# The values of attention groups 2 and 3 as seven block products, and the pooling tiles ahead of these groups' queries and keys

## The chip, the cores and the metric

The kernel runs on one core of one Trainium2 chip. The metric is the device time of one execution in microseconds (us), as the median of several executions. The profile is one execution recorded by the hardware profiler. Engines: PE is TensorE (matrix products), DVE is VectorE, ACT is ScalarE, POOL is GpSimd, SP is SyncE (it issues most of the transfers).

## The reference

One decoder block on 512 tokens of width 1024 in float32: a SwiGLU, a token-mixing layer, a second SwiGLU, each after a norm that is scaled and shifted by a conditioning vector (`w_ada`). The change lies in the token-mixing layer:

```python
proj = u @ w_in                       # u: 512 x 1024
p, q, k, v, gate_logits = split(proj) # widths 256, 768, 768, 768, 2048
y_pool = multiscale_pool(p, ...)      # trailing means over 2, 4, 8, 16 tokens, minus the token
q, k = rope(q), rope(k)               # three head groups of 4 heads x 64, dilations 1, 4, 16
outs, lses = zip(*(dilated_window_attention(q[g], k[g], v[g]) for g in range(3)))
y_attn = sum over groups of softmax(lses)[g] * outs[g]
gates = sigmoid(gate_logits)
merged = g_pool * (y_pool @ w_pool_branch) + g_attn * (y_attn @ w_attn_branch)
return merged @ w_out
```

The reference's head groups are 0, 1 and 2; the words "groups 2 and 3" mean the second and third of them.

## The kernel before

**Products in three parts.** A float32 operand x is held as hi + lo (both in the format fp32r), and a product is three: hi·hi, lo·hi, hi·lo. The activations u are split once (`UH`, `UL`, eight tiles of 128 features by 512 tokens). Weights come in chunks of 128 x 1024 (512 KB) in the order of `plan`. SP issues their transfer into one of three buffers `raw`; ACT writes the high part `whi` (L377) and DVE the low part `wlo` (L389) into a ring. `look`, called ahead of each tile or product, fetches and splits some steps ahead. `take` hands the split chunk to PE.

**Tiles and blocks.** A plain tile of 128 outputs by 512 tokens is 24 matmuls with 512 columns into one bank of PSUM (`mm_tile`, L421 to L423). `blocks` does four such chunks as a 2x2 block product with seven products in place of eight, each of 24 matmuls with 256 columns (L749 to L751 in `gate_duo`). For that it forms sums of weights: two by DVE (`make`, L312) and two by an accumulating transfer that POOL issues (`add`, L320), and sums of blocks of u. Three banks A, B, C take the products: the first result, in A, is copied by ACT to C before the third product goes on accumulating in A.

**The mixing layer (`mix`).** Order of its weight chunks: q and k of group 1, v of group 1; then eight tiles of q and k of groups 2 and 3; two pooling tiles; four chunks of v of groups 2 and 3; then the gates in pairs ("groups" (6), (0), (2), (4) of `GROUPS`, each with seven block products) with the merge products; then `w_out`.

- Each q or k tile is followed by `rope_a`: ACT copies the bank (L1397), SP issues four transfers that swap rows (L1400), DVE multiplies the bank by the cosines (L1401) and so frees it. `rope_b` (two DVE instructions, L1419 and L1423) follows one tile later.
- A row of `w_ada` is one DVE instruction (L448). Such rows are spread over the tiles (`bg`).
- The attention runs beside the tiles (`hooks`): scores (L1456, 16 or 8 matmuls), then on DVE four masked maxima (L1472), on ACT four exponentials (L1477); a step later transposes on PE (L1489) that ACT copies (L1492); a step later the products with the values (L1507) that DVE copies (L1513, L1515). Group 1 has four such steps, here A0 to A3, groups 2 and 3 together four, B0 to B3.
- A pooling tile ends in `pool_diff`: ACT copies the bank (L1582), POOL forms the trailing means (L1588 to L1597).
- The values of groups 2 and 3 are four chunks of 128 tokens by 512 features: 24 matmuls of 512 columns each (L1765 to L1767), copied by DVE (L1768). B1 to B3 run in these.
- Sums of blocks of u for the first gate pair (`mix_sums`): a transfer copies `UH`, one of POOL adds `UL` (L1319, L1322), DVE adds two more (L1326) and combines them (L1337, L1338), ACT and DVE split them (L1330, L1334).
- `gate_duo` for the gate pair 6 stands between the values and the merge. After its fifth product come `pool_map` (L1608, whose result ACT and DVE read, L1612 and L1613) and `at_fT` (L1547). `settle` (L427) is a matmul of 240 columns ahead of some products whose result is not used.

The instructions of each engine run in the order in which the program emits them; there is no planner beside the calls in `mix`.

## Time and profile before

| | us |
|---|---|
| median of 3 runs (lowest to highest) | 968.51 (967.84 to 969.17) |
| the profiled execution | 969.99 |
| its span from first to last instruction | 968.2 |
| values of groups 2 and 3 with their attention steps | 450.95 to 483.98 in the span |
| gate pair 6, seven products | 483.98 to 507.9 |

A row of the timeline reads: start in us, duration in us, engine, line, operation, result<-operands, shapes, count, and in brackets the idle time before it with what ended it. Durations of one engine overlap, so the time that an instruction takes from its queue is the distance from its start to the next start. The busy shares of the page: PE 99%, DVE 87%, ACT 56%, POOL 9%.

### The profile page before, as it was taken

How to read it: one execution, taken by the hardware profiler on the slowest of the kernel's cores; microseconds unless marked ns; L12 is line 12 of the kernel's file. 1: busy time of each engine (PE TensorE's matmuls, PEld its weight loads, DVE VectorE, ACT ScalarE, POOL GpSimd, SP SyncE). 2: the span in 40 equal slices, each digit the busy share in tenths (PEclk: the TensorE clock that was granted, in tenths of full speed). 3: DMA queues.
4: the chain of work that ended last, by engine and by line, in shares of the span. 5: the costliest groups of instructions: out<-in, count | busy, mean ns of one | idle time of the engine just before them, and what ended most of it. 6: DMA issues, size and time to landing. Idle time of an engine off the chain costs nothing.

```text
span 968.2 us, 18169 instructions
## 1 busy us (share of the span) xinstructions
PE 958.5 (99%) x7296; PEld 899.9 (93%) x7296; DVE 840.3 (87%) x1237; ACT 539.3 (56%) x813; POOL 89.8 (9%) x106
## 2 busy tenths in 40 slices
PE   9999999999999999999999999999999999999997
PEld 7888999999999899778889998998999999999997
DVE  7989999899998778787897877989799888989886
ACT  5443666665755553444565453365666747566655
POOL 0000110101010003005510000000101000110002
PEclk9999999999999999999999999999999999999999
DMA  9857785776768648766457445723757666665632
GB/s 353 283 178 257 197 239 156 202 212 153 219 176 246 171 148 238 239 206 188 90 141 199 124 126 207 243 73 104 194 141 198 170 157 167 172 171 143 169 83 88
DMA packets 54087, 174.71 MB, mean 180 GB/s; under 512 B 7793, under 2 KB 10481, under 8 KB 53746
## 3 DMA queue, kind: packets, MB, share of 16 engines
q1 hardware_dynamic: 44416, 141.29, 44.2%
q0 software_dynamic: 9008, 31.72, 18.1%
q8 instruction: 57, 0.93, 0.4%
q10 hardware_dynamic: 578, 0.53, 0.2%
q14 instruction: 28, 0.23, 0.1%
HBM read 135.36 MB, written 2.24 MB: 142 GB/s over the span
## 4 chain that ended last, share of the span: by engine, by line
PE 84%; DVE 7%; DMA 4%; issue 2%; ACT 1%; POOL 0%; SPq 0%; POOLq 0%; DVEq 0%; ACTq 0%
PE bank L750 13%; PE bank L749 12%; PE bank L751 12%; PE bank L421 7%; PE bank L422 7%; PE bank L423 7%; PE bank L1109 4%; PE bank L1108 4%; PE bank L1110 4%; DVE wlo L389 2%; PE bank L2119 2%; PE bank L2121 1%; PE bank L2123 1%; DMA v<-wada 1%; DMA cs<-wada 1%
## 5 line engine op out<-in xcount | busy, mean ns | idle before, releaser
L389 DVE TENSOR_TENSOR wlo<-raw,whi 128x1024 fp32r<-128x1024 f32 (+3 forms) x150 | 166.4, 1118 | 37.7 <-ACT whi L377 37.5
L749 PE MATMUL bank<-UH,whi 128*128 128x256 f32 x672 | 185.7, 276 | 0.0
L750 PE MATMUL bank<-UL,whi 128*128 128x256 f32 x672 | 185.6, 276 | 0.0
L751 PE MATMUL bank<-UH,wlo 128*128 128x256 f32 x672 | 185.6, 276 | 0.0
L389 DVE TENSOR_TENSOR wlo<-X,whi 128x1024 fp32r<-128x1024 f32 (+3 forms) x133 | 142.2, 1082 | 17.8 <-ACT whi L377 17.6
L377 ACT ACTIVATE whi<-raw 128x1024 fp32r<-128x1024 f32 (+3 forms) x150 | 142.6, 964 | 22.1 <-DMA raw<-wf1o 8.4
L377 ACT ACTIVATE whi<-X 128x1024 fp32r<-128x1024 f32 (+3 forms) x133 | 123.0, 946 | 51.0 <-DVE X L312 46.1
L750 PEld LDWEIGHTS bank<-UL,whi 128*128 128x128 f32 x672 | 126.3, 188 | 0.0
L749 PEld LDWEIGHTS bank<-UH,whi 128*128 128x128 f32 x672 | 126.1, 188 | 0.2
L751 PEld LDWEIGHTS bank<-UH,wlo 128*128 128x128 f32 x672 | 126.2, 188 | 0.0
L751 PE MATMUL bank<-SH,wlo 128*128 128x256 f32 x408 | 112.7, 276 | 0.2 <-DVE wlo L389 0.2
L749 PE MATMUL bank<-SH,whi 128*128 128x256 f32 x408 | 112.6, 276 | 0.0
L750 PE MATMUL bank<-SL,whi 128*128 128x256 f32 x408 | 112.6, 276 | 0.0
L421 PE MATMUL bank<-UH,whi 128*128 128x512 f32 (+1 forms) x272 | 93.0, 342 | 0.0
L422 PE MATMUL bank<-UL,whi 128*128 128x512 f32 (+1 forms) x272 | 92.0, 338 | 0.0
L423 PE MATMUL bank<-UH,wlo 128*128 128x512 f32 (+1 forms) x272 | 91.8, 337 | 0.0
L751 PEld LDWEIGHTS bank<-SH,wlo 128*128 128x128 f32 x408 | 76.6, 188 | 0.4 <-DVE wlo L389 0.4
L749 PEld LDWEIGHTS bank<-SH,whi 128*128 128x128 f32 x408 | 76.6, 188 | 0.0
L750 PEld LDWEIGHTS bank<-SL,whi 128*128 128x128 f32 x408 | 76.6, 188 | 0.0
L1108 PE MATMUL bank<-HI,whi 128*128 128x256 f32 x224 | 61.8, 276 | 0.0
L1109 PE MATMUL bank<-HK,whi 128*128 128x256 f32 x224 | 61.8, 276 | 0.0
L1110 PE MATMUL bank<-HI,wlo 128*128 128x256 f32 x224 | 61.8, 276 | 0.0
(406 smaller groups left out, 2410.9 us busy)
## 6 DMA issues: line engine op xcount, KB each, us to landing
raw<-wmix SPq DMA_DIRECT2D x44, 512.0 KB, 4.3
raw<-wf1i SPq DMA_DIRECT2D x32, 512.0 KB, 5.9
raw<-wf2i SPq DMA_DIRECT2D x30, 512.0 KB, 4.3
ada<-wada SPq DMA_DIRECT2D x23, 512.0 KB, 5.2
X<-raw POOLq DMA_DIRECT2D x23, 512.0 KB, 6.0
xs<-wada SPq DMA_DIRECT2D x17, 512.0 KB, 5.3
X<-wf2i SPq DMA_DIRECT2D x14, 512.0 KB, 4.5
X<-wf1i SPq DMA_DIRECT2D x11, 512.0 KB, 4.6
```

The source lines that it names most:

```text
L377: self.nc.scalar.activation(self.hi[:, y], r[:, x], AF.Copy)
L389: self.nc.vector.tensor_tensor(self.lo[:, y], r[:, x], self.hi[:, y], op=OP.subtract)
L421: M(ps, hi, uh, start=start, stop=False)
L422: M(ps, hi, ul, start=False, stop=False)
L423: M(ps, lo, uh, start=False, stop=stop)
L749: M(o, hi, uh, start=start and p == 0 and k == 0, stop=False, skip_group_check=True)
L750: M(o, hi, ul, start=False, stop=False, skip_group_check=True)
L751: M(o, lo, uh, start=False, stop=k == 3, skip_group_check=True)
L1108: M(o, hi, uh, start=start and m % 2 == 0 and k == 0, stop=False, skip_group_check=True)
L1109: M(o, hi, ul, start=False, stop=False, skip_group_check=True)
L1110: M(o, lo, uh, start=False, stop=k == 1, skip_group_check=True)
L2119: M(b, hi, self.UH[k], start=k == 0, stop=False)
```

## The change

1. **Order of chunks.** The two pooling tiles come ahead of the q and k tiles of groups 2 and 3, which are called n0 to n7 here. Their POOL work uses other scratch space.
2. **Values by blocks.** The four v chunks become one `blocks` with seven products of 24 matmuls, 256 columns each (`value_duo`, lines L1834 to L1836 of the changed kernel). u is the stationary operand, the weights move. The bank of n7 is its C.
3. **Sums of u.** All four sums are formed by DVE (L1323), beside the tiles n4 to n7, and serve the values and all gates. The copying and adding transfers are gone.
4. **Attention steps.** B0 starts in the middle of value product 2 (counted from 0), B1 in product 4, B2 in product 6, B3 in the gate product 1; the rest follows in gate products 3 and 5.
5. **Small moves.** No `settle` in the gate pair 6. `pool_map` comes after its last product, `at_fT` after the first product of the next pair, into a bank that `pool_map` used. 56 rows of `w_ada` instead of 59 are done by the end of the q and k tiles, and 60 by the gate pair 6, where `at_merge` (its exponentials) now comes between two uses of the sigmoid.

The core of the diff:

```diff
@@ lay_mix @@
+    for t in range(2):
+        ch.append(_fmajor(w_in, np.arange(t * P, (t + 1) * P)))
     qk(1)
     qk(2)
-    for t in range(2):
-        ch.append(_fmajor(w_in, np.arange(t * P, (t + 1) * P)))
-    for i in range(4):
-        ch.append(v[2 * i:2 * i + 2, :, 256:].transpose(1, 0, 2).reshape(P, -1))
+    for i, c in ((0, 256), (0, 512), (4, 512), (4, 256)):
+        ch.append(v[i:i + 4, :, c:c + 256].transpose(1, 0, 2).reshape(P, -1))
@@ plan @@
-        plain(mx[:20])
+        plain(mx[:16])
+        blocks(mx[16:20], True, 2)
@@ mix @@
+            for t in range(2):
+                self.pool_diff(t, self.mm_tile(hooks(todo.pop(0), [(7, self.bg)])))
...
+            sums = {4: [(7, lambda: u["whole"](0))],
+                    5: [(1, lambda: u["whole"](2)), (4, u["x0"]), (6, lambda: u["hi"](0)), (7, lambda: u["whole"](1))],
+                    6: [(1, u["x2"]), (3, u["x1"]), (5, lambda: u["lo"](0)), (7, lambda: u["whole"](3))],
+                    7: [(0, lambda: u["hi"](1)), (0, lambda: u["hi"](2)), (1, u["x3"]), (3, lambda: u["lo"](2)),
+                        (5, lambda: u["lo"](1))]}
...
+            self.value_duo(p5, {0: rest[0][1], 1: u["last"]}, {2: step(0), 4: step(1), 6: step(2)})
...
+                                 {2: lambda: (self.at_swap(), rows()), 3: clear, 4: self.at_merge, 5: self.bg, 6: third}, {},
+                                 {1: step(3), 3: step(), 5: step()})
...
-        self.merge_out(at, {0: ends, 1: second, 2: lambda: (self.at_high(1), self.at_low(0)), 3: lambda: self.at_low(1)}, ma)
+        self.merge_out(at, {0: lambda: (self.at_fT(spread[0]), self.bg()), 1: ends, 2: second, 3: lambda: (self.at_high(1), self.at_low(0)),
+                            4: lambda: self.at_low(1), 5: self.bg, 6: self.bg}, ma, mp)
@@ mix_sums @@
         def whole(i):
-            ts = slice(0, HT) if i else slice(HT, T)
-            v.tensor_tensor(x[i], *(y.rearrange("p (k t) -> p k t", k=KT)[:, 4:, ts] for y in (self.UHv, self.ULv)), op=OP.add)
+            k, t = ((4, HT), (0, 0), (0, HT), (4, 0))[i]
+            v.tensor_tensor(four(x[i]), *(y[:, k:k + 4, t:t + HT] for y in u), op=OP.add)
@@ value_duo, new @@
+        A, B, C = self.nb(), self.nb(), self.nb()
...
+        for i, (bank, u, start) in enumerate(((A, lambda: blk(0, 0), True), (B, lambda: self.S[0], True),
+                                              (A, lambda: self.S[1], False), (C, lambda: blk(4, 0), False),
+                                              (A, lambda: self.S[2], False), (B, lambda: blk(0, HT), False),
+                                              (A, lambda: blk(4, HT), False))):
+            self.look(3 if i in (0, 2) else 4)
+            w, x = self.take(), u()
+            for c in range(2):
+                o = bank[:, c * 256:c * 256 + 256]
+                for f in within.get(i, ()) if c else ():
+                    f()
...
+            if i == 0:
+                copy(C, A)
+            elif i == 1:
+                copy(p5, B)
+            elif i == 2:
+                copy(self.v23[:, T1, F2], r(A), -1.0)
+            elif i == 3:
+                copy(self.v23[:, T1, F1], r(C))
+            elif i == 4:
+                copy(self.v23[:, T2, F2], r(A), -1.0)
+            elif i == 5:
+                v.tensor_tensor(self.v23[:, T1, F2], self.v23[:, T1, F2], r(B), op=OP.subtract)
+                v.tensor_tensor(self.v23[:, T2, F2], self.v23[:, T2, F2], r(p5), op=OP.subtract)
+            elif i == 6:
+                copy(self.v23[:, T2, F1], r(A))
...
+            if i in beside:
+                beside[i]()
```

How the instructions now stand, at three places. Names: `bank_95`, `bank_96`, `bank_91` are the three banks that tiles and products use in turn, `rt_...` and `tr` the row-swapped copies, `q_` and `k_` queries and keys, `x_`, `uc`, `s_` and a reused `q_3515` sums of u and their parts, `v_3522` the values' tile (its second half also holds a sum of weights), `AR` and `cs` sums of weights.

DVE, from the second half of one k tile's rope to the next tiles, in the kernel before:

```order
L1419 TENSOR_TENSOR rt_4275<-rt_4275,cs 128x512
L1423 TENSOR_TENSOR q_3515<-q_3515,rt_4275 128x512
L448 SCALAR_TENSOR_TENSOR xs,mod<-xs,cond 128x1024
L1401 TENSOR_TENSOR k_3518<-bank_95,cs 128x512
L389 TENSOR_TENSOR wlo<-raw_64,whi 128x1024
L1419 TENSOR_TENSOR rt_4340<-rt_4340,cs 128x512
L1423 TENSOR_TENSOR k_3518<-k_3518,rt_4340 128x512
L448 SCALAR_TENSOR_TENSOR xs,mod<-xs,cond 128x1024
L1401 TENSOR_TENSOR k_3518<-bank_96,cs 128x512
```

and in the changed one, between n6's first rope instructions and the multiplication that frees n7's bank (`bank_95`):

```order
L1416 TENSOR_TENSOR rt_4397<-rt_4397,cs 128x512
L1420 TENSOR_TENSOR q_3517<-q_3517,rt_4397 128x512
L1323 TENSOR_TENSOR q_3515<-UH,UL 128x1024
L1398 TENSOR_TENSOR k_3520<-bank_91,cs 128x512
L390 TENSOR_TENSOR wlo<-v_3522,whi 128x256
L390 TENSOR_TENSOR wlo<-v_3522,whi 128x768
L1335 SCALAR_TENSOR_TENSOR q_3515<-q_3515,x_3501 128x1024
L1331 TENSOR_TENSOR x_4475<-x_3502,v_4463 128x1024
L1331 TENSOR_TENSOR x_4483<-x_3501,k_4461 128x1024
L1416 TENSOR_TENSOR rt_4449<-rt_4449,cs 128x512
L1420 TENSOR_TENSOR k_3520<-k_3520,rt_4449 128x512
L1398 TENSOR_TENSOR k_3520<-bank_95,cs 128x512
```

Where one row of `w_ada` (L448) and one split stood between two multiplications that free a bank (L1401), there are now two splits of a chunk in two pieces, a sum and two splits of sums.

ACT in the changed kernel, from the first bank copy of the values to the third:

```order
L1816 ACTIVATE bank_95<-bank_96 128x512
L378 ACTIVATE whi<-raw_65 128x1024
L378 ACTIVATE whi<-raw_63 128x1024
L1816 ACTIVATE ev<-bank_91 128x512
L1338 ACTIVATE UH<-q_3515 128x4x256
L1474 ACTIVATE prob,st<-prob,negmax 128x256 x4
L1816 ACTIVATE v_3522<-bank_96 128x2x256
L378 ACTIVATE whi<-v_3522 128x1024
```

The copy that empties bank A after product 2 (`v_3522<-bank_96`) stands behind the four exponentials of step B0, and the split of the next chunk behind that copy.

PE in the kernel before, after the fifth product of gate pair 6:

```order
L1608 MATMUL bank_97<-ev,wpool 64x512
L1608 MATMUL bank_93<-ev,wpool 64x512
L1608 MATMUL bank_97<-ev,wpool 64x512
L1608 MATMUL bank_93<-ev,wpool 64x512
L1547 MATMUL bank_94<-cst,f 8x128 x4
```

and in the changed kernel, after its last product, where 24 matmuls of the next pair's first product follow (the first of them is shown):

```order
L754 MATMUL bank_95<-UH,wlo 128x256
L1604 MATMUL bank_94<-ev,wpool 64x512
L1604 MATMUL bank_93<-ev,wpool 64x512
L1604 MATMUL bank_94<-ev,wpool 64x512
L1604 MATMUL bank_93<-ev,wpool 64x512
L752 MATMUL bank_91<-UH,whi 128x256
```

and what comes behind these 24 (the last three of them ahead):

```order
L752 MATMUL bank_91<-UH,whi 128x256
L753 MATMUL bank_91<-UL,whi 128x256
L754 MATMUL bank_91<-UH,wlo 128x256
L1544 MATMUL bank_94<-cst,f 8x128 x4
L428 MATMUL bank_93<-UH,whi 128x240
L752 MATMUL bank_93<-uc,whi 128x256
```

`at_fT` (L1544) and the `settle` behind it (L428) now write the two banks that `pool_map` filled.

## The prediction

> **What bounds the kernel now.** First the page: busy shares, then the chain of work that ended last.

> ```profile
> PE 958.5 (99%) x7296; PEld 899.9 (93%) x7296; DVE 840.3 (87%) x1237; ACT 539.3 (56%) x813; POOL 89.8 (9%) x106
> PE 84%; DVE 7%; DMA 4%; issue 2%; ACT 1%; POOL 0%; SPq 0%; POOLq 0%; DVEq 0%; ACTq 0%
> ```

> PE sets the end, and DVE, busy 87%, is next. The list of PE's waits has seven entries in all; the longest is

> ```profile
> PE bank L2020 <- DVE ones L2025: 1.1, 1, 1.1
> ```

> at the kernel's start; the others are shorter. So a matmul less is time won, and any wait that the change brings to PE is time lost. Next the stretches of 10 us (per engine the busy time and the instructions, then clock, DMA share and GB/s):

> ```profile
> core 0: us, PE busy (x) PEld busy (x) DVE busy (x) ACT busy (x) POOL busy (x), PEclk, DMA share, GB/s
> 410.00:420.00 10.00, 10.00 (x60) 7.83 (x59) 9.86 (x23) 4.51 (x12) 0.00 (x0) 1.00 0.76 242
> 430.00:440.00 10.00, 10.00 (x49) 8.34 (x48) 7.98 (x17) 6.33 (x14) 0.11 (x1) 1.00 0.46 138
> 440.00:450.00 10.00, 10.00 (x66) 7.86 (x65) 6.79 (x14) 1.93 (x2) 4.19 (x3) 1.00 0.70 200
> 450.00:460.00 10.00, 10.00 (x60) 8.24 (x60) 7.95 (x20) 6.78 (x19) 9.43 (x11) 1.00 0.63 194
> ```

> The tiles n4 to n7 of the changed kernel lie between 428 and 450. There DVE has 2.0 to 3.2 us in 10 to spare. That is the resource which the change spends.

> **The matmuls.** Pace is the distance of starts (PE):

> ```profile
> 450.95 0.39 PE L1765 MATMUL bank<-whi,UH 128*128 128x512 f32 x1
> 454.13 0.39 PE L1767 MATMUL bank<-whi,UL 128*128 128x512 f32 x1
> 487.92 0.38 PE L427 MATMUL bank<-UH,whi 128*128 128x240 f32 x1
> 488.14 0.28 PE L749 MATMUL bank<-k,whi 128*128 128x256 f32 x1
> 490.88 0.28 PE L749 MATMUL bank<-k,whi 128*128 128x256 f32 x1
> 502.26 0.28 PE L749 MATMUL bank<-UH,whi 128*128 128x256 f32 x1
> 505.09 0.28 PE L749 MATMUL bank<-UH,whi 128*128 128x256 f32 x1
> ```

> With 512 columns: 14 steps in 3.18 us, 0.227 each. With 256: 24 steps in 2.74 us (0.114) or in 2.83 us (0.118). The four chunks cost 96 x 0.227 = 21.8 us; seven products cost 168 x 0.114 to 0.118 = 19.2 to 19.8. I take the slow pace, since the new products come without a `settle` and behind breaks: 2.0 won, at most 2.6. Two `settle` fewer win 2 x 0.22 = 0.4; if the gate products then all run at the slow pace, 144 x 0.004 = 0.6 is lost. I set these two against each other. **Matmuls: -2.0 us, bounds -3.0 and -1.4.** The attention steps are as many as before, each still one break.

> [...]

> **DVE's account, n4 to the third value product.** These rows give the price of each kind (distance to the next start where DVE went on at once):

> ```profile
> 430.94 0.69 DVE L1419 TENSOR_TENSOR rt<-rt,cs 128x512 f32<-128x512 f32 x1
> 431.67 0.69 DVE L1423 TENSOR_TENSOR q<-q,rt 128x512 f32<-128x512 f32 x1
> 432.27 1.22 DVE L448 SCALAR_TENSOR_TENSOR xs<-xs,cond 128x1024 f32<-128x1024 f32 x1
> 433.42 0.69 DVE L1401 TENSOR_TENSOR k<-bank,cs 128x512 f32<-128x512 f32 x1
> 434.02 1.22 DVE L389 TENSOR_TENSOR wlo<-raw,whi 128x1024 fp32r<-128x1024 f32 x1
> 440.23 1.21 DVE L389 TENSOR_TENSOR wlo<-raw,whi 128x1024 fp32r<-128x1024 f32 x1
> 441.36 1.22 DVE L448 SCALAR_TENSOR_TENSOR xs<-xs,cond 128x1024 f32<-128x1024 f32 x1
> 442.51 0.42 DVE L1515 COPY o<-bank 128x256 f32<-128x256 f32 x1
> 468.90 1.21 DVE L312 TENSOR_TENSOR AR<-raw,raw 128x1024 f32<-128x1024 f32 x1
> 470.14 1.23 DVE L312 TENSOR_TENSOR cs<-raw,AR 128x1024 f32<-128x1024 f32 x1
> ```

> A rope pair (`rope_b`) 1.33, a multiplication that frees a bank 0.60, anything of 1024 columns 1.14, 0.1 more where it needs the one just before. From 430.94 on DVE has to do, in the order of the changed program, up to the multiplication that frees n7's bank: four rope pairs (5.3), four multiplications (2.4), fifteen instructions of 1024 columns (four whole sums, four combinations, three low parts, two sums of weights, two splits: 17.1), a split in two pieces (1.25), a copy of attention values (0.35): 26.4, with 0.1 each at two to four places 26.7, so until 457.6 or so. It can't begin earlier: the maxima of A3 ahead of it wait for PE.

> When does PE want it? Attention steps A fall on the same places, as the pooling tiles only change places with the others. The tile that begins again here is then n6, with 9 matmuls to go and n7's 24 behind:

> ```profile
> 441.00 1.09 PE L1507 MATMUL bank<-probT,v 128*64 128x128 f32 x16
> 442.02 0.50 PE L421 MATMUL bank<-UH,whi 128*128 128x512 f32 x1
> ```

> 442.02 + 33 x 0.227 + 0.1 for the break = 449.6: value product 0; products 1 and 2 at 452.4 and 455.3. Product 2 writes bank A, so ACT must have copied A to C, which is n7's bank, so DVE must have multiplied n7's bank. 457.6, and the copy 0.6 (row below), make 458.2. **Product 2 is 2.9 us late** (2.3 to 3.5).

> A second way to the same: the sums and combinations and their splits add eleven instructions, the two sums of weights two, four rows of `w_ada` go: 9 x 1.14 = 10.3 us more, in 22 us that have about 5.5 to spare. DVE ends nearly 5 us late; one tile of lead covers a part.

> **Behind it.** The queues of ACT and DVE run in order, and the rows are

> ```profile
> 429.07 0.42 DVE L1472 CUSTOM_DVE_ANT_0 prob<-bank,masks 128x256 f32<-128x256 f32 x1 [0.62 <-PE bank L1456]
> 430.14 0.51 ACT L1477 ACTIVATE prob<-prob,negmax 128x256 f32<-128x256 f32 x1 [4.87 <-DVE negmax L1474]
> 432.13 0.67 ACT L1397 ACTIVATE tr<-bank,cst 128x512 f32<-128x512 f32 x1
> 432.70 1.05 ACT L377 ACTIVATE whi<-raw 128x1024 fp32r<-128x1024 f32 x1
> 495.27 0.58 ACT L1814 ACTIVATE k<-bank 128x512 f32<-128x512 f32 x1
> 434.55 1.04 PE L1489 MATMUL bank<-cst,prob 128*128 128x128 f32 x8
> 435.34 0.48 PE L421 MATMUL bank<-UH,whi 128*128 128x512 f32 x1
> 447.69 1.16 PE L1456 MATMUL bank<-k,q 64*128 64x128 f32 x16
> ```

> From the first maximum to the first exponential 1.07, the four exponentials 1.99, a split on ACT 1.05, a copy 0.58; on PE a turn 0.79, scores 1.1.

> - B0's scores, in the middle of product 2, need n7's rope pair. DVE has two splits ahead of it, the second behind an ACT split that follows the copy: 458.2 + 1.0 + 1.1 + 1.4 = 461.7; PE is there at 458.2 + 1.4 + 0.4 = 460.0: **1.7 late** (1.0 to 2.2).
> - Product 4 writes A once ACT has copied product 2. PE is ready at 461.7 + 0.8 + 1.4 + 2.8 = 466.7. The copy stands behind B0's exponentials, these behind two DVE instructions: 461.7 + 2.3 + 1.1 + 2.0 + 0.6 = 467.7: **1.0 late** (0 to 1.5).
> - Product 6: the same with B1. PE: 467.7 + 1.4 + 0.8 + 1.1 + 0.2 + 1.4 + 2.8 = 475.4. The ACT split behind the copy ends at 468.7; six DVE instructions, maxima, exponentials and copy take 6.9 + 1.1 + 2.0 + 0.6: 479.2, or 3.8 late. Where those six need not wait for that split, they begin 2.7 sooner and it is 1.1 late. I take the middle, **2.5**.
> - The values of B0, in product 6, need a subtraction (0.6) behind a split (1.1) behind an ACT split (1.05) behind that copy: 2.8 after it, where PE is there after 1.4: 1.4 late at most, none if the split was ahead: **1.0**.
> - `at_fT` writes a bank of `pool_map`, which DVE must have read.

> ```profile
> 499.13 2.01 PE L1608 MATMUL bank<-ev,wpool 64*64 64x512 f32 x8
> 503.67 1.40 DVE L1613 SCALAR_TENSOR_TENSOR PL<-bank,vecs,xs 128x512 fp32r<-128x512 f32 x2
> 497.76 1.28 ACT L1822 ACT_TABLE_LOAD   x1
> ```

> DVE had read the first bank 5.2 us after `pool_map` began; PE now comes back after 2.0 + 2.8 = 4.8: 0.4 late. A table load (1.3) and two ACT splits (2.1) now stand ahead of the read: 3.8 late at most. **1.7** with the `settle` behind it.

> The sum: 2.9 + 1.7 + 1.0 + 2.5 + 1.0 + 1.7 = 10.8 us of waits, less 2.0: **+8.8 us** (all low ends with the best matmuls +1.8, all high ends with the worst +14.8). The profiled execution took 969.99 (span 968.2 and 1.8 around it), 1.5 above the median of the runs, so 978.8 stands for 977.3 against the median 968.51. Copies, four fewer DVE copies of values, the transfers of u and the moved rows of `w_ada` lie off PE's path: costed at nothing. If a late row of `w_ada` were missed later, it would cost its 1.14.

> **Rivals.**
> 1. *The first waits only.* PE's delay gives DVE and ACT time, and the later steps are hidden: 4.6 - 2.0 = +2.6, 971.1. For it: every microsecond that PE waits is one for DVE. Against it: the exponentials begin after PE's own scores, so the delay moves them along.
> 2. *DVE keeps pace, the change wins.* Place: n7's multiplication; it decides the sign if DVE is there by 454.6, 3 us sooner than the sum. Then B0's scores, exponentials and copies come 3 us sooner too, which clears the waits behind as well, but for 0.4 at `at_fT`: 968.5 - 2.0 + 0.4 = 966.9. For it: before, no wait in this stage at 87% DVE, and POOL no longer runs beside these tiles. Against: the prices come from rows where DVE was not disturbed, and the order is fixed.
> 3. *The pooling takes DVE's time earlier too.* A split took 2.31 beside POOL's work in place of 1.22:

> ```profile
> 470.28 2.23 POOL L1597 TENSOR_TENSOR ev<-ev,v 64x512 f32<-64x512 f32 x1
> 471.29 2.31 DVE L389 TENSOR_TENSOR wlo<-AR,whi 128x1024 fp32r<-128x1024 f32 x1
> ```

> Some three such come to 3.3 us. That work now begins some 50 us sooner and runs into 410 to 420, where DVE is busy 9.86 of 10: 977.3 + 3.3 = 980.6. Against it: 420 to 430 has room to catch up. [...]
> 4. *Nothing comes of it*: half of the chain and no more: within 0.2% of 968.5.

> **How the numbers follow.** The forecast (977.3, about 972.5 to 983) has 0.60, rival 1 0.15, rival 3 0.11, rival 2 0.10, rival 4 0.04. What this kernel's measurement can tell from no change is about 0.2%, 1.9 us. Faster 0.11 (rival 2, a little of 4), slower 0.82 (the forecast, rival 3, three quarters of rival 1), same 0.07. The range leaves out most of rival 2 below and the end of rival 3 above: 967 to 983.

> **What would show it.** In the changed profile: PE's waits name, in value product 2, an ACT copy of bank A, with L1398 on DVE just ahead of it at about 457; in product 2's middle the rope's L1420; in products 4 and 6 the ACT copies L1816; at L1544 the read L1609. DVE busy near 10 of 10 from 430 to 460. Products at 0.118 a matmul. Wrong is the forecast if L1398 on n7's bank ends by 455, or if PE shows no wait between 455 and 480.

## The result, and the profile after

The changed kernel takes 979.62 us (median of 4 runs, 978.68 to 980.78) against 968.84 for the kernel before, measured beside it: the ratio is 1.0111, with a 95% interval from 1.0094 to 1.0129. It is 1.1% slower. The profiled execution took 980.78, with a span of 977.9 against 968.2. Three single executions, of 1613, 2482 and 5501 us, are left out of all medians and ratios.

The page of the changed kernel: busy shares, and the chain that ended last.

```profile
PE 960.6 (98%) x7366; PEld 905.3 (93%) x7366; DVE 850.9 (87%) x1255; ACT 549.4 (56%) x837; POOL 90.8 (9%) x107
PE 84%; DVE 9%; issue 2%; ACT 2%; DMA 2%; POOL 0%; SPq 0%; POOLq 0%; DVEq 0%; ACTq 0%
```

The shares hardly move: 9.7 us of 978 are not seen in them. The list of PE's waits shows where to look (total, times, longest, in us):

```profile
PE bank L1834 <- ACT bank L1816: 4.3, 1, 4.3
PE bank L1834 <- ACT v L1816: 2.3, 1, 2.3
```

Both are new, and both stand in the value products; the longest after them, 1.1 at the kernel's start, was there before. The timeline of PE there (start, duration, in brackets the wait ahead):

```profile
449.61 0.28 PE L1834 MATMUL bank<-whi,UH 128*128 128x256 f32 x1
...
452.43 0.38 PE L1834 MATMUL bank<-whi,uc 128*128 128x256 f32 x1
...
459.75 0.58 PE L1834 MATMUL bank<-whi,k 128*128 128x256 f32 x1 [4.32 <-ACT bank L1816]
...
460.56 0.41 PE L1834 MATMUL bank<-whi,k 128*128 128x256 f32 x1
...
461.20 0.41 PE L1834 MATMUL bank<-whi,k 128*128 128x256 f32 x1
...
462.61 2.08 PE L1453 MATMUL bank<-k,q 64*128 64x128 f32 x16
...
464.62 0.58 PE L1834 MATMUL bank<-whi,k 128*128 128x256 f32 x1
...
479.42 0.58 PE L1834 MATMUL bank<-whi,UH 128*128 128x256 f32 x1 [2.26 <-ACT v L1816]
...
482.27 1.21 PE L1504 MATMUL bank<-probT,v 128*64 128x128 f32 x16
```

Product 0 begins at 449.61 and product 1 2.82 us later, 0.118 a matmul. Then PE stands for 4.32 us ahead of product 2 and for 2.26 ahead of product 6. Behind the first wait three matmuls take 0.64 us (460.56 to 461.20): 0.213 each, nearly twice the time of one before. The stretches of 10 us show the same on DVE's side, and those of 2 us show the clock (the columns are as in the prediction; the last three are the granted clock, the DMA share and GB/s):

```profile
400.00:410.00 10.00, 10.00 (x51) 8.26 (x48) 8.64 (x17) 5.81 (x14) 9.50 (x8) 1.00 0.39 113
410.00:420.00 10.00, 10.00 (x60) 7.77 (x60) 9.90 (x18) 1.73 (x6) 9.28 (x8) 1.00 0.58 188
430.00:440.00 10.00, 10.00 (x50) 8.33 (x49) 9.82 (x21) 5.87 (x14) 0.00 (x0) 1.00 0.31 91
440.00:450.00 10.00, 10.00 (x58) 8.09 (x57) 9.84 (x12) 5.39 (x8) 0.97 (x1) 1.00 0.54 113
450.00:460.00 10.00, 5.68 (x48) 5.45 (x47) 9.93 (x12) 2.49 (x4) 0.89 (x1) 0.93 0.51 124
456.00:458.00 2.00, 0.00 (x0) 0.00 (x0) 1.97 (x3) 0.00 (x0) 0.00 (x0) 1.00 1.03 197
460.00:462.00 2.00, 2.00 (x10) 2.00 (x11) 1.46 (x3) 2.00 (x4) 0.00 (x0) 0.50 0.00 0
464.00:466.00 2.00, 2.00 (x16) 1.78 (x13) 2.00 (x5) 0.00 (x0) 0.00 (x0) 0.63 0.62 193
480.00:482.00 2.00, 2.00 (x11) 2.00 (x10) 1.66 (x2) 1.26 (x2) 0.00 (x0) 0.50 0.00 0
```

From 430 to 460 DVE has no time left (9.8 to 9.9 of 10 are busy, where it had 2.0 to 3.2 to spare before). PE is idle from 456 to 458, and when it comes back its clock is granted at 0.50. The DVE and ACT rows that end the first wait, and the first row that shows DVE late:

```profile
430.25 0.41 DVE L1469 CUSTOM_DVE_ANT_0 prob<-bank,masks 128x256 f32<-128x256 f32 x1
...
458.34 0.68 DVE L1398 TENSOR_TENSOR k<-bank,cs 128x512 f32<-128x512 f32 x1
...
459.12 0.58 ACT L1816 ACTIVATE bank<-bank 128x512 f32<-128x512 f32 x1 [5.83 <-DVE k L1398]
...
462.56 0.69 DVE L1420 TENSOR_TENSOR k<-k,rt 128x512 f32<-128x512 f32 x1
```

A ledger by one stage: from A0's scores to the first merge tile (128x512 matmuls) PE took 142.46 us before (386.07 to 528.53) and takes 152.02 after (385.41 to 537.43), 9.6 more. Two waits make 6.6. Four pieces at the halved clock (half of product 2, B0's scores, the next matmuls, half of product 6) take about 4.2 more than at full pace. An attention turn beside the pooling, from the transposes at 419.84 to the product with the values at 426.85, is 0.6 longer than before (7.0 in place of 6.45). That is 11.4; what is left to the 9.6, 1.8 us, was won on the matmuls. By the medians the whole kernel lost 10.8, so about 1.2 us of the loss lie outside this stage and were not followed. The experiments below are compared by this stage too, since the part of the program ahead of it differs by up to 3.5 us from one execution to the next. Within the stage, the part ahead of product 0 still takes 63.3 to 64.2 us in versions that change nothing there, so differences of less than a microsecond are read from product 0 on: 87.82 us in the changed kernel (449.61 to 537.43).

### The profile page after: what moved, and what is told of

Read it like the earlier page. It is cut to its first block, busy times and chain, and to the rows that moved or that the text cites. A ratio compares the mean times of both kernels' runs of the same rounds, so it can differ in the third digit from the quotient of the medians.

```text
span 977.9 us, 18361 instructions
## 1 busy us (share of the span) xinstructions
PE 960.6 (98%) x7366; PEld 905.3 (93%) x7366; DVE 850.9 (87%) x1255; ACT 549.4 (56%) x837; POOL 90.8 (9%) x107
## 4 chain that ended last, share of the span: by engine, by line
PE 84%; DVE 9%; issue 2%; ACT 2%; DMA 2%; POOL 0%; SPq 0%; POOLq 0%; DVEq 0%; ACTq 0%
PE bank L752 12%; PE bank L753 12%; PE bank L754 12%; PE bank L422 8%; PE bank L423 8%; PE bank L424 8%; PE bank L1112 4%; PE bank L1113 4%; PE bank L1111 4%; DVE wlo L390 2%; PE bank L2123 2%; PE bank L2127 1%; PE bank L2125 1%; DMA cs<-wada 1%; ACT prob L1474 1%
```

## The experiments

### Read n7's bank first

```diff
-                    6: [(1, u["x2"]), (3, u["x1"]), (5, lambda: u["lo"](0)), (7, lambda: u["whole"](3))],
-                    7: [(0, lambda: u["hi"](1)), (0, lambda: u["hi"](2)), (1, u["x3"]), (3, lambda: u["lo"](2)),
-                        (5, lambda: u["lo"](1))]}
+                    6: [(1, u["x2"]), (3, u["x1"]), (5, lambda: u["lo"](0))],
+                    7: [(0, lambda: u["hi"](1)), (0, lambda: u["hi"](2))]}
...
                 rest = [(6, lambda dst=dst, hp=hp, w=rt[1]: self.rope_b(dst, hp, w))]
+            u["lo"](1)
...
-            self.value_duo(p5, {0: rest[0][1], 1: u["last"]}, {2: step(0), 4: step(1), 6: step(2)})
+            self.value_duo(p5, {0: rest[0][1], 2: lambda: (u["whole"](3), u["x3"](), u["lo"](2), u["last"]())}, {2: step(0), 4: step(1), 6: step(2)})
```

> The changed kernel (979.6 us) with another order on DVE: n7's bank is read by L1398 right behind the splits that the tile itself needs; the sums and splits that stood ahead of it (whole(3), x3, lo2) come in value product 2, behind the attention step. No work is added or removed. Theory (DVE has more work between 430 and 470 than PE's time there, so that the lateness only moves): PE's wait ahead of product 2 falls from 4.3 to 1 us or less and TensorE's clock stays full there, but a wait for the split lo2 of some 3 to 6 us comes ahead of product 4, and some 2 to 3 us stay at product 6; the time is 977 to 981 us. Rival (only the place of the read in DVE's order is at fault, later work has room): no wait above 1.5 us after it, 972 to 975 us.

Measured: 977.62, ratio 1.0077 (1.0054 to 1.0101); the stage 150.62. PE's waits in it, by the timeline:

```profile
458.36 0.49 PE L1453 MATMUL bank<-k,q 64*128 64x128 f32 x4 [1.29 <-DVE k L1420]
...
468.85 0.58 PE L1836 MATMUL bank<-whi,x 128*128 128x256 f32 x1 [5.36 <-DVE x L1331]
```

The wait ahead of product 2 is gone, and 5.36 us for lo2 stand ahead of product 4's third matmul. So the lateness is an amount of DVE work, not one badly placed instruction: with the steps where they are, the order moves it. The theory holds in this; the 2 to 3 us that it expected at product 6 did not come, and 0.79 us at B0's values did. From product 0 on 0.8 us were won, since the wait for lo2 took the place of those ahead of products 2 and 6.

### Keep PE busy in the wait

```diff
             w, x = self.take(), u()
+            for _ in range(38 if i == 2 else 0):
+                self.settle(self.bS[0], self.UH[0][:, :P], self.UH[0])
```

> The changed kernel with 38 unused matmuls of 240 columns (about 3.8 us) on PE ahead of value product 2, so that TensorE does not stand idle for 4.3 us before it. Theory (DVE and ACT set the time of B0's scores and of product 4's bank, and the halved clock after the wait hides in waits that would have been there anyway): granted clock 1.00 through product 2, B0's scores then wait about 1 us for the rope, product 4 about 1 us for ACT, product 6 still about 2.3 us; the time falls by 0 to 1 us, 978.6 to 979.8. Rival (the halved clock costs its 2.6 us in full): 976.5 to 977.5 us. A second rival (the clock falls for another reason than the idle PE, such as the load before): the clock is 0.5 to 0.7 in product 2 even so.

Measured: 979.05, ratio 1.0093 (1.0072 to 1.0114); the stage 151.38. It is 0.64 shorter than after, but that lies ahead of product 0, where the two kernels are alike: product 0 began 63.34 us into the stage in place of 64.20, and from there on this version took 88.04 us in place of 87.82. The waits that the timeline now shows:

```profile
462.36 0.49 PE L1453 MATMUL bank<-k,q 64*128 64x128 f32 x4 [1.00 <-DVE k L1420]
...
468.11 0.39 PE L1836 MATMUL bank<-whi,v 128*128 128x256 f32 x1 [0.97 <-ACT v L1816]
...
478.48 0.38 PE L1836 MATMUL bank<-whi,UH 128*128 128x256 f32 x1 [2.41 <-ACT v L1816]
```

and product 2 in the stretches of 2 us:

```profile
459.00:461.00 2.00, 2.00 (x22) 1.87 (x23) 1.46 (x3) 2.00 (x3) 0.00 (x0) 1.00 0.00 0
```

With PE kept busy the clock stays at 1.00 in product 2, so the idle time is what halved it. The whole chain of waits of the prediction then stands in the open: B0's scores 1.00 late, product 4 0.97, product 6 2.41. The halved clock had covered the first two. Behind the first wait it cost nothing that can be measured, against the 2.6 us of the rival: an engine that would have waited anyway loses little by being slow. The clock behind product 6's wait was halved here as before, so what that one costs is not shown by this run.

### Without the trailing means on GpSimd

```diff
-  g.tensor_tensor(o[rows, 2 * w - 1:], src[rows, 2 * w - 1:], src[rows, w - 1:528 - w], op=OP.add)
...
-  g.tensor_tensor(d[rows], d[rows], p[rows, 16:], op=OP.subtract)
+  g.memset(d, 0.0)
```

> The changed kernel with GpSimd's trailing means left out (the difference tiles are set to zero instead, so that the pooled part of the output is left out of the computation); everything else stands in its place. Theory (the pooling beside DVE at 400 to 420 costs DVE about 1.2 us at the beginning of the stage, 429.07 against 430.25 for A3's maxima): n7's bank is read 1.2 us sooner, PE's wait ahead of product 2 is about 3.1 us, the time 977 to 979 us. If 3.1 us of idle time are too short to halve TensorE's clock, up to 1.5 us less: down to 975.5. Rival (the pooling moved ahead is the main cause): the wait is below 1.5 us, the time 974 us or less. Rival (the pooling costs DVE nothing): within 0.5 us of 979.6, the wait 4.3.

This kernel leaves the trailing means out, so its output is not the layer's; only its time is of use.

Measured: 978.22, ratio 1.0078 (1.0050 to 1.0105); the stage 149.54, 2.5 less than after. The profiled execution was the fastest of three (975.82; the others 978.22 and 978.57). The list of PE's waits:

```profile
PE bank L1827 <- ACT bank L1809: 3.1, 1, 3.1
PE bank L1827 <- ACT v L1809: 2.1, 1, 2.1
```

The first wait is 3.1, as the theory had it, so the pooling costs 1.2 us of it. The other 1.3 of the stage lie ahead of product 0, in two attention turns that are 0.8 and 0.6 us shorter. The second, at 420, stands beside the pooling, and without it takes 6.45 us as in the kernel before. The first, at 391, stands ahead of the pooling and was long in the kernel before too, so it is not the pooling's doing. What the pooling does to DVE is seen in the changed kernel's timeline between 405 and 415:

```profile
405.42 2.14 DVE L390 TENSOR_TENSOR wlo<-raw,whi 128x1024 fp32r<-128x1024 f32 x1 [0.26 <-ACT whi L378]
...
406.55 5.61 POOL L1584 TENSOR_TENSOR v<-v 128x525 f32<-128x525 f32 x3
...
407.48 2.08 DVE L449 SCALAR_TENSOR_TENSOR x<-x,cond 128x1024 f32<-128x1024 f32 x1
...
409.49 1.53 DVE L1416 TENSOR_TENSOR rt<-rt,cs 128x512 f32<-128x512 f32 x1
```

Instructions that take 1.22 and 0.69 alone take 2.1 and 1.5. These three lose 2.6 us. At 430 DVE is 1.2 us late, so it had made up for a part. In this run the clock was halved behind the wait of 3.1 us as well (0.50 from 454.6 to 461.4).

### The sums of u on GpSimd

```diff
-  v.tensor_tensor(four(x[i]), *(y[:, k:k + 4, t:t + HT] for y in u), op=OP.add)
+  nc.gpsimd.tensor_tensor(four(x[i]), *(y[:, k:k + 4, t:t + HT] for y in u), op=OP.add)
```

> The changed kernel with the four sums of u (the four instructions called whole) formed by GpSimd instead of DVE. DVE loses 4.6 us of work ahead of n7's read; GpSimd takes about 2.1 us for each. Theory (DVE's added work ahead of n7's read sets the first wait): the wait ahead of product 2 falls by 1 to 4.3 us (less than the 4.6, if DVE's instructions run slower beside GpSimd's, as the split of 2.31 us did, or if a split waits for its chunk to land); the time 975 to 979 us. Rival (the lateness comes from the order of the steps on ACT and DVE behind n7's read, and not from the sums): the first wait falls by as much, but products 4 and 6 give all of it back, 979 to 980.5 us.

Measured: 983.19, ratio 1.0130 (1.0098 to 1.0162); the stage 155.33, 3.3 more than after. Neither the theory nor the rival foresaw a loss. The timeline:

```profile
422.25 5.72 POOL L1323 TENSOR_TENSOR x<-UH,UL 128x1024 f32<-128x1024 f32 x2 [2.63 <-DVE x L449]
...
422.63 3.11 DVE L390 TENSOR_TENSOR wlo<-raw,whi 128x1024 fp32r<-128x1024 f32 x1
...
425.66 2.86 DVE L1416 TENSOR_TENSOR rt<-rt,cs 128x512 f32<-128x512 f32 x1
...
431.11 2.85 DVE L390 TENSOR_TENSOR wlo<-raw,whi 128x1024 fp32r<-128x1024 f32 x1
...
446.12 3.88 DVE L390 TENSOR_TENSOR wlo<-AR,whi 128x1024 fp32r<-128x1024 f32 x1
...
446.19 2.72 POOL L1323 TENSOR_TENSOR q<-UH,UL 128x1024 f32<-128x1024 f32 x1
```

Beside GpSimd's four sums four DVE instructions take 12.7 us in place of 4.35: 8.3 lost for 4.6 moved away. A3's maxima come so late that PE waits 1.4 for their exponentials at a turn, its clock is halved behind that wait too (from 437.68 to 441.10), and n7's bank is nearly as late as ever (a first wait of 3.8). The work was moved to an engine whose sums cost DVE more time than they took off it. One sum took GpSimd 2.7 to 2.9 us, where the expectation had 2.1 (one of 128x527 takes it 1.06 in the kernel before, which comes to 2.1 at 1024 columns).

### Two of the sums by transfers

```diff
+        def copies(i):
+            nc.sync.dma_start(four(x[i]), block(i, u[0]))
+
+        def adds(i):
+            for j in (0, 2):
+                nc.gpsimd.dma_start(four(x[i])[:, j:j + 2], block(i, u[1])[:, j:j + 2], accum_op=OP.add)
...
-            sums = {4: [(7, lambda: u["whole"](0))],
-                    5: [(1, lambda: u["whole"](2)), (4, u["x0"]), (6, lambda: u["hi"](0)), (7, lambda: u["whole"](1))],
-                    6: [(1, u["x2"]), (3, u["x1"]), (5, lambda: u["lo"](0)), (7, lambda: u["whole"](3))],
+            sums = {4: [(3, lambda: u["copies"](1)), (6, lambda: u["adds"](1)), (7, lambda: u["whole"](0))],
+                    5: [(0, lambda: u["copies"](3)), (1, lambda: u["whole"](2)), (3, lambda: u["adds"](3)), (4, u["x0"]), (6, lambda: u["hi"](0))],
+                    6: [(1, u["x2"]), (3, u["x1"]), (5, lambda: u["lo"](0))],
```

> The changed kernel with two of the four sums of u (blocks 1 and 3) formed by transfers as in the kernel before: SP copies the high part, a transfer of POOL adds the low part. DVE loses 2.3 us of work ahead of n7's read, and nothing computes on GpSimd beside it. [...] Rival (any second writer beside DVE costs it as much as it saves): the first wait stays above 3.5 us and the time at 979 us or more.

Measured: 981.69, ratio 1.0123 (1.0100 to 1.0146); the stage 153.37. The first wait grew to 6.0. The author had taken DVE's amount of work ahead of n7's read to set that wait, and expected 1.5 to 2.5 us there and a time of 977 to 978.6; this gain did not come. The rival's numbers did, but not for its reason, for DVE's instructions kept their 1.22 us. The timeline of POOL and DVE:

```profile
446.75 1.21 POOL L1334 DMA_DIRECT2D q<-UL  x1 [5.70 <-PE bank L424]
...
451.50 1.22 POOL L1334 DMA_DIRECT2D q<-UL  x1 [3.53 <-DMA rt<-tr]
...
456.58 1.22 DVE L1346 SCALAR_TENSOR_TENSOR q<-q,x 128x1024 f32<-128x1024 f32 x1 [3.01 <-issue]
```

DVE stands for 3.01 us ahead of x3, with n7's read behind it. The profile names nothing that ended this wait, but the second half of sum 3, which x3 reads, was issued at 451.50 only, and such a transfer took 4.7 us from issue to landing (median of two): 456.2, just ahead of DVE's start. A sum that comes late holds the in-order queue as surely as one that DVE forms itself.

### Other places for the attention steps

```diff
-            self.value_duo(p5, {0: rest[0][1], 1: u["last"]}, {2: step(0), 4: step(1), 6: step(2)})
+            self.value_duo(p5, {0: rest[0][1], 1: u["last"]}, {3: step(0), 5: step(1)})
...
-                                 {2: lambda: (self.at_swap(), rows()), 3: clear, 4: self.at_merge, 5: self.bg, 6: third}, {},
-                                 {1: step(3), 3: step(), 5: step()})
+                                 {3: lambda: (clear(), self.at_swap(), rows()), 5: lambda: (self.at_merge(), self.bg()), 6: third}, {},
+                                 {1: step(2), 2: step(3), 4: step(), 6: step()})
...
-            self.look(3 if i in (0, 2) else 4)
+            if i not in within:
+                self.look(3 if i in (0, 2) else 4)
```

In product 3 `look` is called behind the step, in product 5 behind the subtractions that end it.

> The changed kernel with the attention steps at other places: B0 in the middle of value product 3, B1 in product 5, B2 in gate product 1, B3 in gate product 2, the rest in 4 and 6; in products 3 and 5 the maxima stand ahead of the next chunks' splits on DVE. So the copies of bank A that products 4 and 6 wait for stand ahead of the exponentials on ACT and not behind them. DVE's order up to n7's read is unchanged. Theory (after the first wait, the time is set by A's copies behind the exponentials): the wait of 4.3 us ahead of product 2 and TensorE's halved clock behind it stay, no wait of over 0.3 us at B0's scores and at product 4, at most 1.3 us at product 6, and the time falls by 3 to 6 us to 973.5 to 976.5. Rival (DVE's and ACT's work as a whole sets the time, wherever the steps stand): other waits of together 4 us or more in the gate products or at at_fT take their place, 978 to 981 us.

Measured: 975.14, ratio 1.0050 (1.0032 to 1.0068); the stage 147.64, 4.4 less than after. One wait is left between the values and the merge:

```profile
460.20 0.58 PE L1837 MATMUL bank<-whi,k 128*128 128x256 f32 x1 [4.24 <-ACT bank L1816]
```

Scores, products 4 and 6 and the values wait for nothing above 0.3 us. The later waits came from the copies of bank A behind the exponentials, as the theory says; nothing came in their place.

### The steps, and n7's bank first

```diff
-                    6: [(1, u["x2"]), (3, u["x1"]), (5, lambda: u["lo"](0)), (7, lambda: u["whole"](3))],
-                    7: [(0, lambda: u["hi"](1)), (0, lambda: u["hi"](2)), (1, u["x3"]), (3, lambda: u["lo"](2)),
-                        (5, lambda: u["lo"](1))]}
+                    6: [(1, u["x2"]), (3, u["x1"]), (5, lambda: u["lo"](0))],
+                    7: [(0, lambda: u["hi"](1)), (0, lambda: u["hi"](2))]}
...
                 rest = [(6, lambda dst=dst, hp=hp, w=rt[1]: self.rope_b(dst, hp, w))]
+            for f in (lambda: u["lo"](1), lambda: u["whole"](3), u["x3"], lambda: u["lo"](2)):
+                f()
```

> As s1_steps, and n7's bank is read by DVE ahead of lo1, whole(3), x3 and lo2, which follow it at once. Theory (with the steps one product later DVE has the time between n7's read and B0's maxima): the wait ahead of product 2 falls from 4.3 to 1 us or less, the clock stays full, and of the lateness at most 2.5 us come back, for a split in product 3 or at B0's scores: 970 to 974 us, 2 to 4 us under s1_steps. Rival (as in e1_bank_first, all of it comes back behind): within 1 us of s1_steps.

Measured: 971.81, ratio 1.0024 (1.0014 to 1.0034); the stage 144.39. The waits of the timeline, and the stretch in which the first lies:

```profile
458.72 0.38 PE L1839 MATMUL bank<-wlo,UH 128*128 128x256 f32 x1 [1.90 <-DVE wlo L390]
...
477.61 0.39 PE L752 MATMUL bank<-uc,whi 128*128 128x256 f32 x1 [1.04 <-ACT v L1817]
```

```profile
457.00:462.00 5.00, 3.21 (x30) 2.77 (x31) 4.97 (x6) 1.79 (x3) 0.00 (x0) 1.00 0.23 61
```

The 4.2 us are gone and 2.9 came back, in smaller pieces, and the clock stays full behind them. From product 0 on, the move that gained 0.8 us alone gains 3.1 here. The steps now leave DVE room behind n7's read, and the halved clock behind the first wait, which in s1_steps no later wait covered, is gone too; how much of the gain each makes was not taken apart.

### The same with two sums by transfers

Against the kernel of the last section, with `copies` and `adds` of the transfers' experiment:

```diff
-            sums = {4: [(7, lambda: u["whole"](0))],
-                    5: [(1, lambda: u["whole"](2)), (4, u["x0"]), (6, lambda: u["hi"](0)), (7, lambda: u["whole"](1))],
+            sums = {4: [(3, lambda: u["copies"](1)), (6, lambda: u["adds"](1)), (7, lambda: u["whole"](0))],
+                    5: [(0, lambda: u["copies"](3)), (1, lambda: u["whole"](2)), (3, lambda: u["adds"](3)), (4, u["x0"]), (6, lambda: u["hi"](0))],
...
-            for f in (lambda: u["lo"](1), lambda: u["whole"](3), u["x3"], lambda: u["lo"](2)):
+            for f in (lambda: u["lo"](1), u["x3"], lambda: u["lo"](2)):
```

> As s2_steps_bank, and two of the sums of u formed by transfers, which takes another 2.3 us from DVE. Theory: the waits between value product 2 and product 6 come to 1 to 3 us together instead of 6.6 and a halved clock; 967 to 971.5 us, so about as fast as the kernel before (968.9) or a little faster. Rival (the transfers land too late for x1 and x2, or slow the chunks of weights): a wait of over 2 us for a sum's part at products 1 to 4, the time not below s2_steps_bank.

Measured: 972.24, ratio 1.0025 (1.0014 to 1.0036); the stage 145.19. PE's waits are 0.35 in product 3, 0.59 at B0's scores, 1.11 at product 6 and 0.78 at gate product 1, 2.8 together where 2.9 were. So product 3's wait shrank by 1.55 us, and the lateness came out behind it; the time is not below the version without transfers. The wait of over 2 us for a sum that the rival foresaw did not come (DVE stood 0.24 us ahead of x3), and why 2.3 us less on DVE are worth nothing here stays open.

### One row of `w_ada` moved

```diff
-                b = self.mm_tile(hooks(todo.pop(0), rest + more + sums.get(n, [(7, self.bg)])))
+                b = self.mm_tile(hooks(todo.pop(0), rest + more + sums.get(n, [(7, self.bg)] if n < 3 else [])))
...
-        self.merge_out(at, {..., 3: lambda: (self.at_high(1), self.at_low(0)),
+        self.merge_out(at, {..., 3: lambda: (self.at_high(1), self.at_low(0), self.bg()),
```

> The changed kernel with one row of w_ada (1.2 us on DVE) taken from the k tile n3 and done in the merge stage, where DVE has room. Theory (DVE carries its lateness from 400 to 420 on to n7's read): A3's maxima at 430 and n7's read stand 1 to 1.2 us sooner, PE's wait ahead of product 2 is 3.1 to 3.4 us instead of 4.3, the clock halves there all the same, the time falls by about 1 us to 978 to 979. Rival (DVE makes up for such a delay by 430): the wait stays at 4 us or more.

Measured: 978.69, ratio 1.0107 (1.0091 to 1.0123); the stage 150.96, 1.1 less than after.

```profile
457.89 0.58 PE L1834 MATMUL bank<-whi,k 128*128 128x256 f32 x1 [3.13 <-ACT bank L1816]
...
467.19 0.38 PE L1834 MATMUL bank<-whi,v 128*128 128x256 f32 x1 [0.97 <-ACT v L1816]
```

1.2 us less on DVE at 420 is 1.2 us less of the first wait: DVE carries every bit of lateness from there to n7's read. The clock was full again by 461, and at once product 4's wait shows, with 0.97 us.

### All of it

```diff
-            for f in (lambda: u["lo"](1), lambda: u["whole"](3), u["x3"], lambda: u["lo"](2)):
-                f()
+            u["lo"](1)
...
-            self.value_duo(p5, {0: rest[0][1], 1: u["last"]}, {3: step(0), 5: step(1)})
+            self.value_duo(p5, {0: lambda: (rest[0][1](),u["whole"](3),u["x3"]()), 1: lambda: (u["lo"](2),u["last"]())}, {3: step(0), 5: step(1)})
...
-        self.bi += 2
+        self.banks, self.bi = [C, B, A], 0
```

This is against s2_steps_bank; the row of `w_ada` is moved as in the last section.

> As s2_steps_bank, with three things more: the row of w_ada moved as in v1_row; whole(3), x3 and lo2 behind the splits that value product 3 waits for and behind n7's rope; the gates' first banks are the value products' C, B, A in this order, so that no gate product waits for the copy of value product 6. No matmul is changed. Theory: the waits of s2_steps_bank in value product 3 (1.9 us), at B0's scores (0.3) and at gate product 1 (1.0) fall to 1.5 us together; 968.5 to 970.5 us, 1 to 3 us under s2_steps_bank and within 0.2% of the kernel before. Rival (DVE's work up to B0's maxima is the limit, so the lateness appears again at product 4 or 6 or at the turn of B0): 2.5 us or more there, 971 to 973 us.

Measured: 969.67, ratio 1.0013 (1.0005 to 1.0022); the stage 141.93, half a microsecond less than before the change. PE's waits have no entry in the value products any more; B0's turn is 0.7 longer than the others, and a split is 0.3 late in the next gates. As expected, the time is within 0.2% of the kernel before; but the interval leaves out 1, so this version is still slower, by about 0.1%, though its stage in this one execution is not.

### All of it, with two sums by transfers

```diff
-            sums = {4: [(7, lambda: u["whole"](0))],
-                    5: [(1, lambda: u["whole"](2)), (4, u["x0"]), (6, lambda: u["hi"](0)), (7, lambda: u["whole"](1))],
+            sums = {4: [(3, lambda: u["copies"](1)), (6, lambda: u["copies"](3)), (7, lambda: u["adds"](1, 0)), (7, lambda: u["adds"](3, 0)), (7, lambda: u["whole"](0))],
+                    5: [(0, lambda: u["adds"](1, 2)), (0, lambda: u["adds"](3, 2)), (1, lambda: u["whole"](2)), (4, u["x0"]), (6, lambda: u["hi"](0))],
...
+            u["x3"]()
...
-            self.value_duo(p5, {0: lambda: (rest[0][1](),u["whole"](3),u["x3"]()), 1: lambda: (u["lo"](2),u["last"]())}, {3: step(0), 5: step(1)})
+            self.value_duo(p5, {0: lambda: (rest[0][1](),), 1: lambda: (u["lo"](2),u["last"]())}, {3: step(0), 5: step(1)})
```

> As v2_all, with the sums 1 and 3 formed by transfers that are issued sooner than in d1_two_dma, in the order 1, 3, 1, 3 of their halves, so that no half waits for the other of the same sum. Theory: the sums land by 448, 2.3 us of DVE's work ahead of n7's read are gone, the waits from value product 0 to gate product 1 come to 1 us or less together; 967 to 969 us, at or under the kernel before. Rival (the transfers still land late or hold up the chunks of weights): DVE waits for a sum behind n7's rope and the time is not below v2_all.

Measured: 971.14, ratio 1.0025 (1.0013 to 1.0037); the stage 143.40. The high part of sum 3 was issued 9 us sooner than in d1_two_dma. Still DVE waits, now for sum 1:

```profile
448.68 1.23 DVE L1344 TENSOR_TENSOR x<-x,x 128x1024 f32<-128x1024 f32 x1 [4.00 <-DMA x<-UL]
```

The four halves went out at 434.9, 439.8, 444.6 and 449.1, one by one, though neighbours go to different tiles; in this order sum 1 ends 5 us later than in d1_two_dma. The rival holds.

### All of it, with the last split later

```diff
-            nc.scalar.activation(old[0], four(x[3]), AF.Copy)
-            sub(old[1], four(x[3]), old[0])
+            if n == 0:
+                nc.scalar.activation(old[0], four(x[3]), AF.Copy)
+            else:
+                sub(old[1], four(x[3]), old[0])
...
-            self.value_duo(p5, {0: lambda: (rest[0][1](),u["whole"](3),u["x3"]()), 1: lambda: (u["lo"](2),u["last"]())}, {3: step(0), 5: step(1)})
+            self.value_duo(p5, {0: lambda: (rest[0][1](),u["whole"](3),u["x3"]()), 1: lambda: (u["lo"](2), u["last"](0))}, {3: step(0) + [lambda: u["last"](1)], 5: step(1)})
...
             do()
             self.bg()
+            self.bg()
             bs = [self.nb(), self.nb()]
```

> As v2_all, with two small moves: the last split of the sums of u on DVE (1.1 us) stands behind B0's maxima and not ahead of them; the moved row of w_ada is done behind the last gates, beside the products with w_out, and not in the merge stage, where a split was 0.3 us late. Theory: the turn of B0 in product 5, 1.7 us long in v2_all in place of 1.0, loses its 0.7 us, the later split its 0.3; 968.5 to 969.3 us, within 0.2% of the kernel before. Rival (the split is then late for product 5): a wait of 0.5 us or more at L1841 in product 5 and no gain on v2_all (969.5 us or more).

Measured: 969.90, ratio 1.0006 (0.9994 to 1.0018); the stage 142.28.

```profile
465.39 0.39 PE L1841 MATMUL bank<-whi,UL 128*128 128x256 f32 x1 [1.32 <-DVE UL L1334]
```

B0's turn lost its 0.7 us, and the split behind the maxima was 1.32 late for product 5, as the rival said. The split that was 0.3 late in the gates is so no longer. v4_last can't be told from the kernel before, v2_all is 0.1% slower; between these two the difference is within the noise. None was found that beats the kernel before.

## Why the prediction was right

The forecast was 977.3 and slower; 979.62 was measured, 2.3 above it and inside the range. Step by step:

- **What bounds.** Right: PE, with DVE's time from 430 to 450 as the resource that the change spends. DVE went from 8.0 and 6.8 to 9.8 of 10 in these two stretches.
- **The matmuls.** Product 0 ran at a pace of 0.118, as said. It came at 449.61, where 449.6 was worked out, but that this agrees so well is chance: the stage began 0.66 sooner than in the kernel before (385.41 against 386.07), and the turn at 420 took 0.6 longer. v2_all and v4_last, with hardly a wait left, put the gain at 1.4 to 1.9 us, by their stages less the waits and the long turns that remain. The -2.0 was a little too good and inside its bounds.
- **DVE's account and product 2.** The mechanism is as described, down to the lines. The size is off: 4.3 late where 2.9 was said. The term at fault is the starting point, 430.94, which was taken from the undisturbed kernel. DVE began 1.2 us later (A3's maxima at 430.25 in place of 429.07), because the pooling beside 400 to 420 had held it up. That was rival 3, whose loss is real (e5_no_pool) but worth 1.2 us at product 2 and 0.6 at the turn at 420, not 3.3. Without the pooling the wait was 3.1, near the 2.9 of the forecast, and one row less gave 3.1 as well. The amount of DVE work was right: 26.8 us from the first rope pair (432.11) to the end of the read that frees n7's bank (458.94), where 26.7 was added up.
- **B0's scores, product 4, product 6.** Said 1.7, 1.0 and 2.5. In the profile after only product 6 shows, with 2.3. With PE kept busy in the first wait all three show: 1.0, 1.0 and 2.4. So the chain was read rightly, and s1_steps shows its cause by undoing it. What the prediction did not see is the halved clock, which slowed PE into these waits, cost nothing measurable beyond them behind the first wait, and ran behind product 6's as well.
- **The values of B0.** 1.0 was said. Their place in the changed kernel is behind a half product at the halved clock, which covered it. In e6_sums_pool and d1_two_dma, where that half ran at the full clock, the list of PE's waits has 0.8 for it.
- **`at_fT`.** Said 1.7; there was no wait. This step failed:

```profile
512.29 1.28 ACT L1781 ACT_TABLE_LOAD   x1
...
513.08 2.01 PE L1604 MATMUL bank<-ev,wpool 64*64 64x512 f32 x8
...
516.31 1.40 DVE L1609 SCALAR_TENSOR_TENSOR x<-bank,vecs,k 128x512 fp32r<-128x512 f32 x2
...
518.04 1.04 PE L1544 MATMUL bank<-cst,f 128*8 128x128 f32 x8
```

  The table load and the two ACT splits, which the prediction put ahead of the read as a delay, began before `pool_map` did, and DVE was through with the first bank (517.05, the first of the two instructions) 4.0 us after `pool_map` began, a microsecond ahead of PE.

By the sum: waits of 10.8 were forecast. 6.6 came as waits and some 4.2 as slow matmuls, with 0.6 at a turn: 11.4, less 1.8. That the sum fits so well is in part luck, since a term that was missing (the clock) took the place of terms that it hid, and the 1.7 for `at_fT`, which never came, made up for most of what was missing at product 2 and at the turn.

## What to carry to other kernels

Where the second engine has 20 to 30% to spare on average, add up its work up to the first instruction that frees a bank, starting from where it really stands at that point with its neighbours' work, and then follow what queues behind. DVE's lateness was here an amount and not a place: with one read moved ahead it showed elsewhere (4.32 us ahead of product 2 became 5.36 ahead of product 4's third matmul in e1_bank_first), and it shrank with work taken off DVE (1.2 us for one row in v1_row) or lost its later waits with their other ends moved back, as the attention steps were (4.4 us in s1_steps). A few matmuls saved are soon spent: 2 us won on PE were paid with 10 us of DVE work in a stretch that had 5.

## What the hardware showed that was not expected

```profile
482.00:485.00 3.00, 2.02 (x16) 1.65 (x16) 1.23 (x2) 2.68 (x5) 0.00 (x0) 1.00 0.05 14
```

The idle time of a window does not decide it alone: one with 1.54 us was followed by the halved clock (at 437.68 in e6_sums_pool), one with 1.74 was not (at 465.2 in e1_bank_first). In these eight runs the clock, once halved, came back after a window with at most 0.57 us idle and stayed down after one with 0.91 to 1.78. What else goes into it was not shown.

**Beside GpSimd's 128x1024 sums DVE instructions took from more than twice to about four times their time** in e6_sums_pool: 2.85, 3.11 and 3.88 us for 1.22, and 2.86 for 0.69. GpSimd's last two sums there ended at 432.88 and 448.91, and the DVE splits beside them 1.08 and 1.09 us later, of the 1.22 that such a split takes alone.

**Accumulating transfers of POOL went out one after the other.** Four of 256 KB each were issued 4.4 to 4.9 us apart in v3_all_dma. What holds them back was not tried, and stays open.
